# Two blocks of a network in one kernel: position tables stored with their keys backwards and read from a single DRAM copy

## The chip, the cores and the metric

The kernel runs on one core of a Trainium2 chip. The metric is the device time of one execution in microseconds. The core has five instruction streams: PE (matmuls; its weight loads are shown as PEld), DVE (elementwise work), ACT (activations, copies), POOL (small elementwise work; it also issues the DMAs of one queue) and SP (issues the DMAs of another). All DMAs share 16 DMA engines.

## The reference, cut to what matters

The program computes two blocks on 256 tokens of width 2048, in float32: a hybrid layer applied twice, then a second block with neighbourhood attention, four branches and a feed-forward part. The change touches only the attention biases, which depend on the distance between query and key.

In the first block, heads add a bias per distance to the scores and mask out later keys:

```python
dist = q_pos[:, None] - k_pos[None, :]
bias = bias_dist[jnp.clip(dist, 0, S - 1)]
s = s + jnp.transpose(bias, (2, 0, 1))[None, :, None]
s = jnp.where(dist >= 0, s, -jnp.inf)
```

So the bias of query q and key k is a function of q - k alone: the table of 128 queries by 256 keys holds one row of 384 values, shifted by one from each query to the next. There are 12 such rows (4 heads of one kind of attention, 8 of another). In the second block's neighbourhood attention, a head has a small table `rpb` by row and column distance; on a grid 64 columns wide its row of 127 values per row distance is shifted by one from each query column to the next in the same way.

## The kernel before, in words

Everything is arranged around a stream of weights. Each step of the program handles one piece of a weight matrix, 256 rows by 512 columns (512 KB). SP loads the piece into one of four `raw` buffers (line 335). ACT rounds it into `hi` (line 343), DVE takes `lo` = `raw` - `hi` (line 351), and PE multiplies with both halves: 12 matmuls of 128x512 a step, for two tiles of 128 tokens (lines 392 to 394). `hi` and `lo` are made up to four steps ahead of their use. A `raw` buffer is free for the next load when `lo` has been computed.

All else (attention heads, a depthwise convolution on DVE, norms, and a long matrix-vector product on DVE called `wmod`) is emitted as side tasks, a link per step, between the matmuls. The emission order is fixed when the program is built; each engine works through its own stream in order and waits on semaphores. A planner decides how much DVE work goes into a step: `Meter` (lines 55 to 76) adds up estimated times from the free sizes of the operands, and `room()` (line 177) says what is left in the step. The DMAs that POOL issues run as soon as POOL comes to them and their waits allow, which can be long before PE gets to that step.

The tables of the first block are made in `bias_tables`, a task that starts at step 20. A small matmul and an addition (line 548) give `r`, the 12 rows of 384 values. Line 551 writes them to DRAM 128 times over. Lines 553 to 556 read three tiles `T` of 4 heads each: partition p takes 256 values from copy p, starting one value earlier than partition p - 1. Such a DRAM row stands with key order ascending:

```python
scr = self.dp.tile([12, 128, 384], F32, name="scr")
nc.gpsimd.dma_start(scr, r.unsqueeze(1).broadcast_to([12, 128, 384]))
    nc.gpsimd.dma_start(t, bass.AP(scr.tensor, g * 4 * 128 * 384 + 127, [[383, 128], [128 * 384, 4], [1, 256]]))
```

The T loads wait for the landing of the write. `T` is used in `causal` (lines 841 and 843), where DVE adds it to the scores in PSUM and takes the minimum, twice per set of scores (256 and 128 columns).

For the second block, the function `tables` at step 220 (lines 1060 to 1064) copies the 56 rows of `rpb` 64 times over from DRAM to DRAM, and then loads a mask. In `na_head` each head has four small loads from that copy in two pairs (line 1261), and DVE subtracts the loaded values from the mask (line 1287).

Of the kernel before, what the change touches and what calls it, by code (L numbers as in the profile page):

```python
# [11 lines left out]
F32 = mybir.dt.float32  # L12
# [3 lines left out]
ALU = mybir.AluOpType  # L16
# [15 lines left out]
TAIL, END = 5, 3  # L32
# the order in which the normed (group, token tile) pieces are transposed, and how many a group's use waits for
TILES = [(0, 0), (1, 0), (0, 1), (1, 1), (2, 0), (2, 1), (3, 0), (3, 1)]
READY = [3, 4, 6, 8]
# the part of the program (in steps) over which each chunk of the modulation's product is spread
WMOD_STEPS = {0: (22, 146), 1: (160, 274), 3: (290, 380), 4: (380, 470), 2: (470, 552), 5: (552, 612)}
# [17 lines left out]
class Meter:  # L55
    """Passes calls on to an engine and adds up about how long they hold it, in us."""

# [29 lines left out]
class Task:  # L87
    """A generator that emits a side chain of the program, a link per step."""

# [23 lines left out]
class Block:  # L113
    """One block of output columns: all of its contraction, for its token tiles."""

# [13 lines left out]
class Kernel:  # L129
# [20 lines left out]

# [1 line left out]
    def s(self, shape, dt=F32, name="s"):  # L152
# [14 lines left out]

# [1 line left out]
    def add(self, gen, front=False, rows=2, banks=1):  # L169
# [7 lines left out]
    def room(self):  # L177
        """Time left on the vector engine until the tensor engine is through this step."""
        return self.t_pe + 2.6 - self.t_dve
# [4 lines left out]
    def need(self, t, items=1 << 30):  # L184
        """Emits what is left of a task (or its first items). A task between steps holds no more than
        its `rows` of the row buffers and its `banks` of the four, and what has begun stays within them."""
        if t.done or t.items >= items:
            return
        if t in self.tasks:
            self.tasks.remove(t)  # L190
        if t not in self.running:
            while self.held()[0] + t.rows > ROWS or self.held()[1] + t.banks > 4:
                self.need([r for r in self.running if not r.busy][0])
            self.running.append(t)
        was, t.forced = t.forced, True
        while not t.done and t.items < items:
            t.step()
        t.forced = was
        if t.done:
            self.running.remove(t)  # L200

    def wait(self, me, deps):
        """Lets steps pass until the tasks are done."""
        while not all(t.done for t in deps):
            if me().forced:
                for t in deps:
                    self.need(t)
                break
            yield
# [12 lines left out]

# [1 line left out]
    def rstd(self, var, n, scale, eps):  # L224
        """(var * scale + eps) ** -0.5 for [128, n]."""
        nc = self.nc
        r = self.m([128, 8], name="rstd", bufs=8)
        nc.gpsimd.tensor_scalar(r[:, 0:n], var, scale, eps, op0=ALU.mult, op1=ALU.add)
        nc.gpsimd.tensor_tensor(r[:, 0:n], r[:, 0:n], self.half[:, 0:n], op=ALU.pow)  # L229
        return r  # L230

    def split_t(self, items, ahead=0):
        """Transposes [128 tokens, 512] pieces and splits them. items: (src, hi, lo, scale, bias),
        src a function that gives the piece; scale and bias: [128, 4] columns or None."""
        nc = self.nc
        n = 0
# [64 lines left out]

# [1 line left out]
    def block(self, *args, **kw):  # L303
# [3 lines left out]
    def order(jobs):  # L307
        """Steps of four (job, half of its contraction, token tile) each, and the step after which each job's
        operands are free. At the tail of a block its first token tile goes ahead of the second."""
        units, i = [], 0  # L310
# [93 lines left out]

# [1 line left out]
    def wmod_init(self):  # L406
        """silu(c) @ w_mod + b_mod on the vector engine, 128 of its elements at a time."""
        self.wm_jobs = [(chunk, f, k) for chunk in (0, 1, 3, 4, 2, 5) for f in range(16) for k in range(2)]
# [95 lines left out]

# [1 line left out]
    def begin(self, load):  # L506
# [27 lines left out]
    def bias_tables(self):  # L534
# [9 lines left out]
        p = self.aux()  # L544
# [3 lines left out]
        nc.vector.tensor_tensor(r, p[0:12, 0:384], mk, op=ALU.add)  # L548
        # 128 copies of each row, read one short of their pitch: row p comes out shifted by p
        scr = self.dp.tile([12, 128, 384], F32, name="scr")  # L550
        nc.gpsimd.dma_start(scr, r.unsqueeze(1).broadcast_to([12, 128, 384]))
        self.T = []
        for g in (1, 2, 0):
            t = self.s([128, 4, 256], name="T")
            nc.gpsimd.dma_start(t, bass.AP(scr.tensor, g * 4 * 128 * 384 + 127, [[383, 128], [128 * 384, 4], [1, 256]]))
            self.T.append(t)
        self.T = [self.T[2], self.T[0], self.T[1]]

# [1 line left out]
    def layer(self, l):  # L560
# [217 lines left out]
    def rms_t(self, r, ss, sc, sh, dst=None, rs=None):  # L778
        """rms norm, scale and shift of token-major r (4 of [128, 2, 512]) into transposed halves."""
        nc = self.nc  # L780
# [37 lines left out]
    def qk_t(self, q, k, c, scale):  # L818
        """Transposed q (times scale) and k of one head: [128, 512], q then k."""
        nc = self.nc  # L820
# [13 lines left out]
    def causal(self, qk, rows, T, s, m, i):  # L834
        """Negated scores of both query tiles: [128, 384] (tile 1, then tile 0) and their minima."""
        nc = self.nc
# [3 lines left out]
        yield  # L840
        nc.vector.tensor_tensor_reduce(out=s[:, 0:256], in0=p[:, 0:256], in1=T, scale=1.0, scalar=3e38,
                                       op0=ALU.add, op1=ALU.min, accum_out=m[:, i:i + 1])
        nc.vector.tensor_tensor_reduce(out=s[:, 256:384], in0=p[:, 256:384], in1=T[:, 128:256], scale=1.0, scalar=3e38,
                                       op0=ALU.add, op1=ALU.min, accum_out=m[:, i + 1:i + 2])
# [9 lines left out]
    def pv(self, s, v, c):  # L854
        """Probabilities [128, 384] times v: PSUM [128, 256], tile 1 then tile 0."""
        nc = self.nc
# [130 lines left out]

# [1 line left out]
    def second(self):  # L989
# [70 lines left out]
        def tables():  # L1060
            self.rpb = self.dp.tile([56, 64, 127], F32, name="rpbs")
            nc.gpsimd.dma_start(self.rpb, a["rpb"].unsqueeze(1).broadcast_to([56, 64, 127]))
            self.mask = self.cp.tile([128, 64], F32, name="namask")
            nc.gpsimd.dma_start(self.mask, a["namask"])
# [168 lines left out]
    def context(self):  # L1233
        """Normed and modulated context, transposed and split."""
        nc, a = self.nc, self.a
# [13 lines left out]
    def na_head(self, j, hd, x, y, need, me):  # L1249
# [7 lines left out]
        def load(t):  # L1257
            raw = self.h([128, 256], name="rpb")
            for i in range(2):
                off = (hd * 7 + 3 - 2 * t - i) * 64 * 127 + 63  # L1260
                nc.gpsimd.dma_start(raw[i * 64:(i + 1) * 64, :].rearrange("p (a c) -> p a c", a=4),
                                    bass.AP(self.rpb.tensor, off, [[126, 64], [64 * 127, 4], [1, 64]]))
            return raw
# [15 lines left out]
        for t in range(2):  # L1279
# [8 lines left out]
                                    self.mask.unsqueeze(1).broadcast_to([128, 4, 64]),  # L1288
                                    raw.rearrange("p (a c) -> p a c", a=4), op=ALU.subtract)
            if t == 0:  # L1290
# [25 lines left out]
    def put_split(self, p, dst, c, scale=None):  # L1316
        """[128, 256] in PSUM into the halves of chunk c."""
        nc = self.nc
# [111 lines left out]

# [1 line left out]
def _bucket(d):  # L1432
# [6 lines left out]
def _constants():  # L1439
# [4 lines left out]
    oh[_bucket(np.maximum(d, 0)), j] = -1.0  # L1444
    c["onehot"] = oh
    mask = np.zeros((12, 384), np.float32)
    mask[:4] = np.where(d >= 0, 0.0, BIG)
    cnt = np.where(d >= 0, (d <= 128) + 1.0 * (d % 4 == 0) + 1.0 * (d % 16 == 0), 0.0)
    mask[4:] = np.where(cnt > 0, -np.log(np.maximum(cnt, 1.0)), BIG)
    c["dmask"] = mask  # L1450
    cc = np.arange(64)
# [20 lines left out]
def _layout(i):  # L1472
# [22 lines left out]
    def blocks(w):  # L1495
        """[.., K, N] as [.., N / 512, K / 256, 128, 1024]: what one transfer brings, in one piece."""
        k, m = w.shape[-2:]
# [8 lines left out]
        "dlam": n["diff_lambda"].reshape(DEPTH, 256), "gain": n["diff_head_gain"], "cols": cols,  # L1506
        "ln_g": n["ln_g"], "ln_b": n["ln_b"], "rel_bias": n["rel_bias"], "rpb": rpb.reshape(56, 127),
        "ctx": n["ctx_2"][0], "c": np.stack([n["c_2"][0], n["c_ctx_2"]]), "w_in2": blocks(n["w_in_2"][0]),
# [24 lines left out]
```

## Time and profile before

| | |
|---|---|
| device time, median of 3 runs | 2675.42 us (2675.05 to 2678.34) |
| profiled execution, first to last instruction (the span) | 2668.7 us; the page gives no other time for it |
| busy: PE, DVE, ACT, POOL | 2624.8, 1843.7, 1260.4, 126.1 us |
| `lo` (DVE, line 351), `hi` (ACT, line 343) | 1220 and 1059 ns each, 893 times |
| DMA moved | 616.79 MB, 231 GB/s over the span |
| DMA queue q0 (issued by POOL) | 11744 packets, 39.29 MB |
| time in DMA from issue to landing, a weight load | 4.4 us median |

Times in the rows below are microseconds from the start of the span unless marked ns. A matmul in the trace shows some 0.39 us because it overlaps with its neighbours; the distance from one start to the next is what it costs. The chain of work that ended last is followed back from the last instruction, at each step to what released it. Most of PE's matmuls have one line in the trace (line 75, the planner's wrapper), so they are told apart by tiles: `mm` is the weight stream, `aux` are the side tasks.

### The profile page before, as it was taken

What the parts mean: (1) busy time and instruction counts of PE and PEld (TensorE: products, weight loads), DVE (VectorE), ACT (ScalarE), POOL (GpSimd) and SP (SyncE); (2) the same over time, 40 slices, a digit from 0 to 9 for tenths busy, and PEclk for the clock granted to TensorE, in tenths of its full rate; (3) what the DMA queues carried; (4) which work ended last, traced back from release to release, by engine and by line L of the source; (5) the groups of instructions that cost most, each with busy time, mean ns of one, the idle gap of its engine ahead of it and who ended that gap; (6) DMA issues with size and microseconds to landing.
All of it is one profiled execution on the core that took longest, in us unless ns stands there. A gap on an engine that the chain in (4) does not pass through costs nothing.

```text
span 2668.7 us, 33167 instructions
## 1 busy us (share of the span) xinstructions
PE 2624.8 (98%) x11962; PEld 2164.3 (81%) x11962; DVE 1843.7 (69%) x3028; ACT 1260.4 (47%) x1609; POOL 126.1 (5%) x188
## 2 busy tenths in 40 slices
PE   9999999989999999999999999999999999999999
PEld 7788888768888888887888888888788888888887
DVE  5699787769988799664756686778554554555444
ACT  6354654435566556454454444444444434443442
POOL 0000010000000111020200000000100000000000
PEclk9999999999999999999999999999999999999999
DMA  8876667577765778785767787788655566556654
GB/s 304 213 231 219 212 225 251 194 221 233 233 227 195 280 268 286 255 256 184 230 224 237 255 283 260 262 289 305 222 181 190 190 237 205 189 190 240 225 194 154
DMA packets 171749, 616.79 MB, mean 231 GB/s; under 512 B 19994, under 2 KB 20788, under 8 KB 171584
## 3 DMA queue, kind: packets, MB, share of 16 engines
q1 hardware_dynamic: 158400, 572.59, 64.0%
q0 software_dynamic: 11744, 39.29, 5.3%
q10 hardware_dynamic: 1440, 2.79, 0.3%
q8 instruction: 94, 1.54, 0.2%
q14 instruction: 71, 0.58, 0.1%
HBM read 599.64 MB, written 16.76 MB: 231 GB/s over the span
## 4 chain that ended last, share of the span: by engine, by line
PE 87%; DVE 5%; DMA 4%; issue 2%; ACT 1%; POOL 0%; SPq 0%; ACTq 0%; DVEq 0%; POOLq 0%
PE mm L75 82%; PE aux L75 6%; DMA raw<-in_w_in 3%; DVE lo L351 2%; DVE f L75 1%; DVE wmjunk L75 1%; DVE cacc L75 1%; DMA raw<-in_w_out 1%; ACT hi L343 0%; DVE res L75 0%; DMA row<-in_ln_b 0%; DMA row<-in_ln_g 0%; DVE hcTl L75 0%; POOL rstd L229 0%; DVE bn L75 0%
## 5 line engine op out<-in xcount | busy, mean ns | idle before, releaser
L351 DVE TENSOR_TENSOR lo<-raw,hi 128x1024 fp32r<-128x1024 f32 (+1 forms) x893 | 1077.0, 1220 | 629.9 <-ACT hi L343 627.2
L343 ACT ACTIVATE hi<-raw 128x1024 fp32r<-128x1024 f32 (+1 forms) x893 | 937.5, 1059 | 1067.4 <-PE mm L75 777.7
L75 PE MATMUL mm<-hi,xTh 128*128 128x512 f32 x960 | 388.0, 404 | 18.3 <-ACT hi L343 18.3
L75 PE MATMUL mm<-lo,xTh 128*128 128x512 f32 x960 | 379.0, 395 | 3.5 <-DVE lo L351 3.5
L75 PE MATMUL mm<-hi,xTl 128*128 128x512 f32 x960 | 379.1, 395 | 0.6 <-DVE xTl L75 0.6
L75 DVE CUSTOM_DVE_ANT_0 wmjunk<-wm,c 128x512 bf16<-128x512 f32 x512 | 352.9, 689 | 13.1 <-DMA wm<-in_w_mod 1.9
L75 PE MATMUL mm<-hi,hTh 128*128 128x512 f32 x864 | 343.9, 398 | 0.0
L75 PE MATMUL mm<-hi,hTl 128*128 128x512 f32 x864 | 337.1, 390 | 0.0
L75 PE MATMUL mm<-lo,hTh 128*128 128x512 f32 x864 | 336.6, 390 | 0.0
L75 PE MATMUL mm<-hi,h2Th 128*128 128x512 f32 x704 | 275.9, 392 | 1.1 <-ACT h2Th L284 1.1
L75 PE MATMUL mm<-hi,h2Tl 128*128 128x512 f32 x704 | 274.4, 390 | 1.1 <-DVE h2Tl L75 1.1
L75 PE MATMUL mm<-lo,h2Th 128*128 128x512 f32 x704 | 274.2, 389 | 0.0
L75 PEld LDWEIGHTS mm<-hi,xTh 128*128 128x128 f32 x960 | 183.0, 191 | 57.9 <-ACT hi L343 20.0
L75 PEld LDWEIGHTS mm<-lo,xTh 128*128 128x128 f32 x960 | 183.2, 191 | 42.0 <-DVE lo L351 6.4
L75 PEld LDWEIGHTS mm<-hi,xTl 128*128 128x128 f32 x960 | 182.6, 190 | 40.5 <-DVE xTl L75 1.3
L75 PEld LDWEIGHTS mm<-hi,hTl 128*128 128x128 f32 x864 | 162.2, 188 | 34.5
L75 PEld LDWEIGHTS mm<-lo,hTh 128*128 128x128 f32 x864 | 162.5, 188 | 32.4 <-issue 0.2
L75 PEld LDWEIGHTS mm<-hi,hTh 128*128 128x128 f32 x864 | 162.4, 188 | 32.3 <-issue 0.2
L75 PEld LDWEIGHTS mm<-hi,h2Tl 128*128 128x128 f32 x704 | 132.2, 188 | 29.0 <-DVE h2Tl L75 1.5
L75 PEld LDWEIGHTS mm<-hi,h2Th 128*128 128x128 f32 x704 | 132.2, 188 | 28.3 <-ACT h2Th L284 1.6
L75 PEld LDWEIGHTS mm<-lo,h2Th 128*128 128x128 f32 x704 | 132.3, 188 | 26.9
L75 PE MATMUL mm<-hi,yTh 128*128 128x512 f32 x384 | 151.2, 394 | 0.0
(273 smaller groups left out, 3094.9 us busy)
## 6 DMA issues: line engine op xcount, KB each, us to landing
raw<-in_w_in SPq DMA_DIRECT2D x360, 512.0 KB, 4.4
wm<-in_w_mod SPq DMA_DIRECT2D x192, 512.0 KB, 4.7
raw<-in_w_gate SPq DMA_DIRECT2D x128, 512.0 KB, 4.5
raw<-in_w_fg SPq DMA_DIRECT2D x88, 512.0 KB, 4.3
raw<-in_w_fu SPq DMA_DIRECT2D x88, 512.0 KB, 3.9
raw<-in_w_fd SPq DMA_DIRECT2D x88, 512.0 KB, 4.2
raw<-in_w_out SPq DMA_DIRECT2D x64, 512.0 KB, 4.6
raw<-in_w_o SPq DMA_DIRECT2D x32, 512.0 KB, 5.1
```

The source lines that it names most:

```text
L75: return f(*args, **kw)
L343: nc.scalar.activation(hi[:, k], t[:, k], AF.Copy)
L351: nc.nc.vector.tensor_tensor(lo[:, k], t[:, k], hi[:, k], op=ALU.subtract)
```

## The change: what it does

The 12 rows and the `rpb` rows are stored with their keys backwards. Then the row of partition p starts one value *later* than that of partition p - 1, and 128 overlapping reads of one DRAM row, a step of one value apart, give the shifted table; a pitch of 383 over 128 copies is no longer needed. `scr` is 12 rows of 384 values (18 KB); the copy of `rpb` is dropped and the loads of `na_head` read the input itself. The tables in SBUF now hold their keys backwards, so DVE reads them with a step of -1 in three places. The constants (`onehot`, `dmask`) and `rpb` are reversed when the inputs are laid out. Comments are gone as well, which changes no instruction.

```diff
-        scr = self.dp.tile([12, 128, 384], F32, name="scr")
-        nc.gpsimd.dma_start(scr, r.unsqueeze(1).broadcast_to([12, 128, 384]))
+        scr = self.dp.tile([12, 384], F32, name="scr")
+        nc.gpsimd.dma_start(scr, r)
...
-            nc.gpsimd.dma_start(t, bass.AP(scr.tensor, g * 4 * 128 * 384 + 127, [[383, 128], [128 * 384, 4], [1, 256]]))
+            nc.gpsimd.dma_start(t, bass.AP(scr.tensor, g * 4 * 384 + 1, [[1, 128], [384, 4], [1, 256]]))
...
-        nc.vector.tensor_tensor_reduce(out=s[:, 0:256], in0=p[:, 0:256], in1=T, scale=1.0, scalar=3e38,
+        nc.vector.tensor_tensor_reduce(out=s[:, 0:256], in0=p[:, 0:256], in1=T[:, ::-1], scale=1.0, scalar=3e38,
...
-        nc.vector.tensor_tensor_reduce(out=s[:, 256:384], in0=p[:, 256:384], in1=T[:, 128:256], scale=1.0, scalar=3e38,
+        nc.vector.tensor_tensor_reduce(out=s[:, 256:384], in0=p[:, 256:384], in1=T[:, 0:128][:, ::-1], scale=1.0, scalar=3e38,
...
-            self.rpb = self.dp.tile([56, 64, 127], F32, name="rpbs")
-            nc.gpsimd.dma_start(self.rpb, a["rpb"].unsqueeze(1).broadcast_to([56, 64, 127]))
...
-                off = (hd * 7 + 3 - 2 * t - i) * 64 * 127 + 63
+                off = (hd * 7 + 3 - 2 * t - i) * 127
...
-                                    bass.AP(self.rpb.tensor, off, [[126, 64], [64 * 127, 4], [1, 64]]))
+                                    bass.AP(a["rpb"].tensor, off, [[1, 64], [127, 4], [1, 64]]))
...
-                                    raw.rearrange("p (a c) -> p a c", a=4), op=ALU.subtract)
+                                    raw.rearrange("p (a c) -> p a c", a=4)[:, :, ::-1], op=ALU.subtract)
...
-    c["onehot"] = oh
+    c["onehot"] = oh[:, ::-1]
...
-    c["dmask"] = mask
+    c["dmask"] = mask[:, ::-1]
```

## Rows read from the trace of the kernel before

**Rows 1.** The head of the page: span, then busy us of each engine.

```profile
span 2668.7 us, 33167 instructions
PE 2624.8 (98%) x11962; PEld 2164.3 (81%) x11962; DVE 1843.7 (69%) x3028; ACT 1260.4 (47%) x1609; POOL 126.1 (5%) x188
```

**Rows 2.** Timeline of PE, first stretch: start us, us, engine, line, operation, idle before.

```profile
75.74 0.39 PE L75 MATMUL mm<-lo,xTh 128*128 128x512 f32 x1
...
98.41 0.39 PE L75 MATMUL mm<-hi,xTl 128*128 128x512 f32 x1
99.89 0.50 PE L75 MATMUL mm<-hi,xTh 128*128 128x512 f32 x1 [1.10 <-ACT hi L343]
...
114.28 0.40 PE L75 MATMUL mm<-hi,xTl 128*128 128x512 f32 x1
```

**Rows 3.** The chain of work that ended last: start us, us, what.

```profile
84.80 26.66 DMA raw<-in_w_in
113.91 7.33 DMA raw<-in_w_in
565.53 25.66 DMA raw<-in_w_in
```

**Rows 4.** DMA issues: out<-in, queue, count, KB each, median us to landing.

```profile
c<-in_c ACTq DMA_DIRECT2D x4, 512.0 KB, 11.0
scr<-r POOLq DMA_DIRECT2D x1, 2304.0 KB, 36.4
rpb<-rpbs POOLq DMA_DIRECT2D x32, 64.0 KB, 5.7
rpbs<-in_rpb POOLq DMA_DIRECT2D x1, 1778.0 KB, 30.5
T<-scr POOLq DMA_DIRECT2D x3, 512.0 KB, 5.7
mk<-in_dmask POOLq DMA_DIRECT2D x1, 18.0 KB, 5.9
```

**Rows 5.** Instructions on `scr` and `rpbs`: duration ns min/median/max, first and last start.

```profile
L551 POOL DMA_DIRECT2D scr<-r x1: 1108/1108/1108, 75.3 to 75.3; - x1
...
L1062 POOL DMA_DIRECT2D rpbs<-in_rpb x1: 1718/1718/1718, 560.3 to 560.3; - x1
```

**Rows 6.** Busy us of PE, PEld, DVE, ACT, POOL; clock, DMA share, GB/s.

```profile
90.00:95.00 5.00, 5.00 (x23) 4.13 (x22) 2.02 (x3) 1.06 (x1) 0.00 (x0) 1.00 0.80 139
```

**Rows 7.** Timeline of PE, second stretch, columns as in rows 2.

```profile
578.93 0.39 PE L75 MATMUL mm<-hi,xTl 128*128 128x512 f32 x1
588.57 0.80 PE L75 MATMUL mm<-hi,xTh 128*128 128x512 f32 x1 [9.26 <-ACT hi L343]
...
593.73 0.40 PE L75 MATMUL mm<-hi,xTl 128*128 128x512 f32 x1
```

**Rows 8.** Timeline of PE, later places in the two layers, columns as in rows 2.

```profile
127.45 0.39 PE L75 MATMUL mm<-hi,xTh 128*128 128x512 f32 x1
128.46 0.50 PE L75 MATMUL mm<-lo,xTh 128*128 128x512 f32 x1 [0.62 <-DVE lo L351]
...
153.27 0.39 PE L75 MATMUL mm<-hi,xTl 128*128 128x512 f32 x1
...
156.33 0.48 PE L75 MATMUL mm<-hi,xTh 128*128 128x512 f32 x1
...
641.09 0.39 PE L75 MATMUL mm<-hi,xTl 128*128 128x512 f32 x1
...
642.59 0.48 PE L75 MATMUL mm<-hi,xTh 128*128 128x512 f32 x1
```

**Rows 9.** Instructions on tiles `sc`, `rpb`: ns min/median/max, first and last start, shapes.

```profile
L75 DVE CUSTOM_DVE_ANT_0 sc<-aux,T x64: 282/352/425, 153.0 to 849.0; 128x256 f32<-128x256 f32 x32, 128x128 f32<-128x128 f32 x32
L75 DVE TENSOR_SCALAR f<-aux,sc,sh x64: 389/397/408, 1014.1 to 1944.2; 128x128 f32<-128x128 f32 x64
...
L75 DVE TENSOR_TENSOR pad<-namask,rpb x16: 414/418/427, 1150.1 to 1410.5; 128x256 f32<-128x256 f32 x16
```

More of the change, by code (lines that the diff above doesn't have):

```diff
@@ L1506, in _layout @@
         "dlam": n["diff_lambda"].reshape(DEPTH, 256), "gain": n["diff_head_gain"], "cols": cols,
-        "ln_g": n["ln_g"], "ln_b": n["ln_b"], "rel_bias": n["rel_bias"], "rpb": rpb.reshape(56, 127),
+        "ln_g": n["ln_g"], "ln_b": n["ln_b"], "rel_bias": n["rel_bias"], "rpb": rpb[:, :, ::-1].reshape(56, 127),
         "ctx": n["ctx_2"][0], "c": np.stack([n["c_2"][0], n["c_ctx_2"]]), "w_in2": blocks(n["w_in_2"][0]),
```

## The prediction

> **What bounds the kernel now.** I read the head of the page first, then the chain that ended last, then the DMA issues, then the PE timeline around the places that stood out. PE is busy for 98% of the 2668.7 us span while DVE has 69% [rows 1], so a change off PE can only gain where PE is starved. Its steady rhythm is one 128x512 matmul every 0.2267 us: from the start at 75.74 to the one at 98.41 there are 100 intervals, 22.67 us [rows 2].
>
> The chain names two long links that are not PE: a weight load in flight for 26.66 us from 84.80, and another for 25.66 us from 565.53 [rows 3]. The DMA issues and their times say what else was in flight. The broadcast write `scr<-r` (2304 KB) goes out at 75.3 [rows 5] and takes 36.4 us, so to about 111.7; the weight load lands at 84.80 + 26.66 = 111.46. The broadcast write `rpbs<-in_rpb` (1778 KB) goes out at 560.3 [rows 5] and takes 30.5 us, to 590.8; the weight load lands at 591.19 [rows 3, 4]. Each pair agrees within half a microsecond; that is my evidence that these DRAM copies clog the engines that the weights share. While one is under way the DMA engines are 0.80 busy and move 139 GB/s in all, and DVE works 2.02 us of 5 [rows 6].
>
> What PE loses. First stretch: the last matmul on rhythm starts at 98.41, then 27 start late, the first at 99.89 and the last at 114.28; on rhythm the 27th would start at 98.41 + 27 x 0.2267 = 104.53, so 9.75 us are lost. Second stretch: 578.93 is on rhythm, 12 follow from 588.57 to 593.73, and on rhythm the 12th would start at 578.93 + 2.72 = 581.65: 12.08 us lost [rows 2, 7]. The lower clock during the restarts is inside both figures.
>
> **Part by part.**
>
> *The 128-fold copy goes.* `scr` becomes 18 KB. Its write costs about what the 18 KB load of the mask does, 5.9 us instead of 36.4 [rows 4], with twelve rows in place of 1536. The first clog vanishes, and with it 9.75 us. POOL's wait for the landing shrinks with it; nothing but the conv's later `rstd` is queued behind that wait on POOL, so it gives and costs nothing by itself.
>
> *The 64-fold copy goes.* One DMA of 1778 KB and the POOL slot that issues it go; the mask load behind it on the same queue lands sooner. The second clog vanishes: 12.08 us.
>
> *What follows the first clog.* After it DVE has lost its lead and PE pays twice more. A matmul at 128.46 follows one at 127.45, 0.78 over rhythm. Then nine transposes of the first heads' probabilities come late: from 153.27 to 156.33 is 3.06 us between the neighbouring matmuls, while the same nine in the second layer take 641.09 to 642.59, 1.50 us; 1.56 us over [rows 8]. Both are lateness of DVE, which stood idle more than half the time under the clog [rows 6]. Without the clog it keeps its lead, so I count both, 2.34 us; the other end is 0, if DVE would have been late anyway. The second layer's follow-up I put at 0, since that layer's transposes run undelayed already.
>
> *The three T loads move forward by about 30 us*, from the write's landing at 111.7 to about 75.3 + 1.1 + 5.9 = 82 [rows 4, 5]. Their sizes stay, 1 KB runs into 128 partitions, 1.5 MB together. What is new is that all of it is read from one region of 18 KB, and that it now falls beside weight loads that are in no distress yet. Their cost is not shown, so by bounds. Below: nothing, as the loads, where they stand now, land in 5.7 us and the weight load beside them in 7.33 us from 113.91 [rows 3, 4], and PE keeps its rhythm until 127.45. The cover is what the first clog shows: a weight load issued at 84.80 was not missed by PE before 98.64, 13.84 us later, less the two conversions. 7.33 us is well under it. Above: the slowest moving of such bulk on this queue, the `rpbs` write's 1778 KB in 30.5 us = 58 GB/s, which makes 1536 KB last 26.3 us. The row nearest in kind is `c<-in_c`: four loads of 512 KB, each reading one 4 KB row of DRAM for all 128 partitions, land in 11.0 us [rows 4], so a hot source as such does not choke the engines. I take 0. T is first used at 153.0 [rows 9], 60 us after it would land.
>
> *The 32 `rpb` loads* keep their size (64 KB, 256-byte runs, 5.7 us [rows 4]) and their place; they read 28 KB of DRAM in place of 1.8 MB. First use of the values is at 1150.1 [rows 9], behind PE work; 0 by the same argument.
>
> *The reversed operand.* 64 `sc` instructions (half of 256 columns, half of 128; median 0.352 us) and 16 `pad` instructions (256 columns, 0.418 us) now read one input backwards [rows 9]: 32 x 256 + 32 x 128 + 16 x 256 = 16384 columns, 64 x 0.352 + 16 x 0.418 = 29.2 us of DVE. No row has a negative step. Below: 0, the same words in the same number of columns; a gain I exclude, since nothing is read less. Above: the slowest float32 row per column, `f<-aux,sc,sh`, 128 columns in 0.397 us or 3.10 ns each [rows 9]; at that pace 16384 columns take 50.8 us, 21.6 more. I take 0, since the operands stay dense float32 of the same shapes. The program's own planner counts free sizes alone, so the order of instructions on each engine stays as it is.
>
> [...]
>
> **The sum.** 9.75 + 12.08 + 2.34 = 24.2 us, on the profiled execution's span: 2668.7 - 24.2 = 2644.5. That span lies 6.7 us under the 2675.42 us median of the runs shown (what is before the first and after the last instruction); I keep that as it is: 2651.2 us. What is late next is DVE: it is nearly full after each clog, but it no longer starts there with nothing in hand.
>
> **The rivals.**
>
> [...]
>
> *B. The T loads, read from one small region, clog in their turn.* From the two clogs: the losses plus the cover, 9.75 + 13.84 over 36.4 us and 12.08 + 13.6 over 30.5 us, are 0.65 and 0.84 us per us of clog; I take 0.75, so a clog of C us costs 0.75 C - 13.7. At the 58 GB/s pace C = 26.3 and 6.0 us come back: 2657.2. Against: the `c` loads.
>
> *C. Slower: the same place at the worst pace.* An `rpb` load moves 64 KB in 5.7 us, 11.2 KB per us. If reads of one DRAM spot go no faster however many are asked for, 1536 KB last 137 us: 0.75 x 137 - 13.7 = 89 us, 2740. It outweighs the gain as soon as C passes (24.2 + 13.7) / 0.75 = 51 us, that is under 30 KB per us for the T loads. The `c` loads, 2048 KB with a median landing of 11.0 us, speak strongly against it.
>
> *D. The change doesn't do what it says:* the weight loads are late for another reason (buffers freed late by DVE, whose work stands in the chain just ahead of both links), and the writes only happen to end together with them. Then 2675. Against: two landings that agree within half a microsecond, and 139 GB/s at 0.80 busy.
>
> **How the numbers follow.** Forecast as summed 0.68, with a range of its own of 2647 to 2655 (2.34 us less gained, and some 3 us either way for the estimate); A 0.13, B 0.10, C 0.04, D 0.05. The range 2646 to 2662 takes in the likeliest, B, and A up to half its upper end. About 0.2%, 5.4 us, is what a measurement of this kernel can tell from no change: faster by more holds in the forecast, A and B, 0.91; D is within, 0.05; C is slower, 0.04.
>
> **What would show it.** Right: no weight load of 20 us or more in the chain; `scr<-r` landing within about 6 us; no PE gap over 1 us between 85 and 160 or between 565 and 645; the nine transposes of the first layer within about 1.5 us; later events of the first layer about 12 us earlier, of the second about 24. [...] I am wrong if PE still stops for weights in those stretches, or if the gain at about 200 us is kept but lost again behind DVE by 900 us.

## The result, and the profile after

The changed kernel takes 2647.68 us (median; 2646.82 to 2648.27) against 2675.83 us (2675.05 to 2678.34) beside it: 28.15 us less, ratio 0.9897, 95% interval 0.9882 to 0.9911. The forecast was 2651.2 us, 24.2 us less. The profiled execution has a span of 2646.2 us and a time of 2647.96 us.

The head of the page, to be held against [rows 1]: PE's share of the span has gone from 98% to 99%.

```profile
span 2646.2 us, 33166 instructions
PE 2615.5 (99%) x11962; PEld 2161.0 (82%) x11962; DVE 1843.9 (70%) x3028; ACT 1260.5 (48%) x1609; POOL 125.1 (5%) x187
```

The chain that ended last, at the two places of [rows 3] (start us, us, what): where weight loads of 26 us stood, PE follows on PE.

```profile
71.22 49.21 PE mm L75 x216
...
537.37 57.15 PE mm L75 x252
```

The DMA issues that answer to [rows 4] (KB each, median us to landing). The two copies are gone, and the mask that was queued behind the second lands in 4.0 us. The T loads take 11.0 us instead of 5.7.

```profile
rpb<-in_rpb POOLq DMA_DIRECT2D x32, 64.0 KB, 5.7
T<-scr POOLq DMA_DIRECT2D x3, 512.0 KB, 11.0
namask<-in_namask POOLq DMA_DIRECT2D x1, 32.0 KB, 4.0
scr<-r POOLq DMA_DIRECT2D x1, 18.0 KB, 3.4
```

The mask's line before:

```profile
namask<-in_namask POOLq DMA_DIRECT2D x1, 32.0 KB, 29.3
```

Busy us of PE, PEld, DVE, ACT, POOL, then clock, DMA share and GB/s, in the stretches where the T loads now fall. In [rows 6] the DMA engines moved 139 GB/s at a share of 0.80; here they move 382 and 385 at 1.02 and 1.01, and PE is full.

```profile
85.00:90.00 5.00, 5.00 (x24) 4.14 (x23) 3.29 (x6) 1.97 (x2) 0.00 (x0) 1.00 1.02 382
90.00:95.00 5.00, 5.00 (x24) 4.14 (x23) 3.10 (x4) 1.21 (x2) 0.00 (x0) 1.00 1.01 385
```

The weight loads beside the T loads do take longer than their median of 4.4 us: the eight that are issued between 77 and 97 us land in 3.6 to 9.9 us, median 6.8.

PE at the nine transposes of [rows 8] (start us, us): from 142.42 to 143.55 is 1.13 us between the matmuls around them, where it was 3.06. DVE is ahead again: its first instruction on these scores starts at 135.4, 7.2 us before the transposes; before the change it started at 153.0 [rows 9], 1.1 us before the first of them.

```profile
142.42 0.40 PE L75 MATMUL mm<-hi,xTl 128*128 128x512 f32 x1
142.65 1.14 PE L75 MATMUL aux<-ident,sc 128*128 128x128 f32 x9
143.55 0.47 PE L75 MATMUL mm<-hi,xTh 128*128 128x512 f32 x1
```

The instructions that read backwards, to be held against [rows 9] (ns min/median/max): unchanged to within 2 ns in the median.

```profile
L75 DVE CUSTOM_DVE_ANT_0 sc<-aux,T x64: 282/352/426, 135.4 to 824.1; 128x256 f32<-128x256 f32 x32, 128x128 f32<-128x128 f32 x32
...
L75 DVE TENSOR_TENSOR pad<-namask,rpb x16: 415/420/426, 1128.9 to 1388.1; 128x256 f32<-128x256 f32 x16
```

Milestones show where the time came from. Three runs of matmuls stand in the chain of each kernel here: one of 60 in the attention of the first layer, its twin in the second layer, and one of 468 at the start of the second block. Before, and after:

```profile
362.96 13.65 PE mm L75 x60
849.22 13.65 PE mm L75 x60
1030.64 106.12 PE mm L75 x468
```

```profile
350.17 13.65 PE mm L75 x60
824.27 13.65 PE mm L75 x60
1008.17 106.12 PE mm L75 x468
```

The first comes 12.79 us earlier, the second 24.95, the third 22.47. Each clog gave 12 to 13 us; then this execution loses 2.48 us between the second layer and the second block, and keeps the rest to the end.

### The profile page after: what moved, and what is told of

The parts are those of the page before. It is cut to its first block, busy times and chain, and to the rows that moved or that the text cites. A ratio compares the mean times of both kernels' runs of the same rounds, so it can differ in the third digit from the quotient of the medians.

```text
span 2646.2 us, 33166 instructions
## 1 busy us (share of the span) xinstructions
PE 2615.5 (99%) x11962; PEld 2161.0 (82%) x11962; DVE 1843.9 (70%) x3028; ACT 1260.5 (48%) x1609; POOL 125.1 (5%) x187
## 4 chain that ended last, share of the span: by engine, by line
PE 92%; DVE 3%; DMA 2%; issue 1%; ACT 1%; POOL 0%; SPq 0%; ACTq 0%; DVEq 0%; POOLq 0%
PE mm L75 86%; PE aux L75 6%; DVE lo L351 1%; DMA raw<-in_w_out 1%; DMA raw<-in_w_in 1%; DVE f L75 1%; DMA row<-in_ln_b 1%; ACT hi L343 0%; DVE res L75 0%; DVE wmjunk L75 0%; POOL rstd L229 0%; DVE hcTl L75 0%; DVE bn L75 0%; POOL rstd L228 0%; DVE yTl L75 0%
## 5 line engine op out<-in xcount | busy, mean ns | idle before, releaser
L75 PE MATMUL mm<-hi,yTl 128*128 128x512 f32 x384 | 149.9, 390 | 1.6 <-DVE yTl L75 1.6
```

The costliest lines, as they stand in the source:

```text
L75: return f(*args, **kw)
```

## Experiments

Ratios are against the kernel before, run on the same chip.

**The kernel before again.** No edit.

> The kernel before, unchanged, to see where 4 of the measured 28 us sit that the sum (24.2 us) did not have: the change's own execution has only 1.8 us around its span, while 6.7 us lay between the span of the profile before and the median of its runs. Theory 1 (the clogs vary): the span of this execution is about 2673 to 2675 us, and PE loses some 28 us rather than 24 in the two stretches where the weight loads are late. Theory 2 (what lies around the span differs by the kernel): the span is again 2668 to 2669 us and the time 2675.

The profiled execution has a span of 2669.2 us and a time of 2670.92: theory 2 falls, 1.7 us lie around the span as in the changed kernel. But theory 1 isn't shown in this trace either. This execution is among the lowest of its ten (2670.59 to 2682.07, median 2674.17; the runs of the kernel before in the same session span 2669.62 to 2683.24), with the clogs at 36.2 and 31.2 us. So both profiles of this kernel show it some 3 to 5 us under its own median, and what an ordinary execution loses more isn't in them. The run with backwards copies, below, has a trace of an ordinary one.

**One table at a time.** The first kernel has the edits of `bias_tables` and `causal` alone, the second those of `tables` and `na_head` alone.

> Only the first block's table is changed (12 rows once in DRAM, read backwards); the 64-fold copy of rpb stays. The clog theory expects half the gain: some 12 to 14 us under the kernel before (ratio 0.995), no PE gap between 85 and 160 us, and the gap of about 12 us near 570 us unchanged. If buffers freed late by DVE were the cause, the time stays within 3 us of the kernel before.

> Only the second block's table is changed (rpb read from the input, backwards); the 128-fold copy stays. The clog theory expects 12 to 15 us under the kernel before (ratio 0.995), the gap after 98 us as before and none near 580 us; with the run that has the other half the gains should add up to that of the whole change within 3 us. The rival of late buffers expects no change of over 3 us.

The first: 2662.18 us (2657.80 to 2665.61), ratio 0.9950 (0.9935 to 0.9965). The second: 2661.16 us (2659.46 to 2665.19), ratio 0.9950 (0.9935 to 0.9964). Against 2674.79 beside them that is 12.6 and 13.6 us less, 26.2 together; the whole change gave 28.15 in its own session and 26.2 in a later one. The chain of each keeps the one long weight load whose copy it keeps (first table only, then second only):

```profile
549.30 23.56 DMA raw<-in_w_in
```

```profile
85.13 27.61 DMA raw<-in_w_in
```

PE doesn't wait at all between 60 and 165 us in the first, and waits 0.6 us in all between 540 and 650 in the second. The two parts are independent and add up within the 3 us that were expected.

**Copies that nobody reads.** The changed kernel and

```diff
+        junk = self.dp.tile([12, 128, 384], F32, name="junk")
+        nc.gpsimd.dma_start(junk, r.unsqueeze(1).broadcast_to([12, 128, 384]))
...
+            self.rpb = self.dp.tile([56, 64, 127], F32, name="rpbs")
+            nc.gpsimd.dma_start(self.rpb, a["rpb"].unsqueeze(1).broadcast_to([56, 64, 127]))
```

> The changed kernel with both broadcast writes put back into DRAM tiles that nothing reads (2304 KB and 1778 KB); the tables are still read from the single copies. The clog theory expects nearly all of the gain to go: within 5 us of the kernel before. If the gain came from what the loads wait for or read (T earlier, reads from a small region), it expects to stay within 3 us of the changed kernel, 28 us faster.

2675.62 us (2670.78 to 2680.06), ratio 1.0003 (0.9993 to 1.0012): all of the gain goes, with nothing that depends on the copies. The copies alone are the cost. The first stretch costs somewhat more than before (the first milestone stands at 365.84, where the kernel before has 362.96); the T loads now queue behind the copy and land in 36.4 us, which is the likely reason. In its windows PE starves as before:

```profile
95.00:100.00 5.00, 4.39 (x20) 3.30 (x18) 0.00 (x0) 0.00 (x0) 0.00 (x0) 1.00 0.80 152
100.00:105.00 5.00, 0.64 (x1) 0.29 (x1) 0.67 (x1) 1.06 (x1) 0.00 (x0) 0.77 0.78 126
```

**Backwards, with the copies.** The changed kernel with both folds kept, and the pitch one longer instead of one shorter. Cut to the read of the first table; the `rpb` loads are changed in the same way:

```diff
...
-            nc.gpsimd.dma_start(t, bass.AP(scr.tensor, g * 4 * 384 + 1, [[1, 128], [384, 4], [1, 256]]))
+            nc.gpsimd.dma_start(t, bass.AP(scr.tensor, g * 4 * 128 * 384 + 1, [[385, 128], [128 * 384, 4], [1, 256]]))
...
```

> Keys backwards and the three reversed reads on DVE as in the change, but both folds of copies kept in DRAM (read with a pitch one longer instead of one shorter). If the whole gain is the copies, the time is that of the kernel before, within 4 us, and the DVE instructions on T and on the rpb values keep 0.35 and 0.42 us. [...]

2674.65 us (2670.88 to 2677.65), ratio 1.0002 (0.9992 to 1.0012). The reversed instructions have medians of 350 and 419 ns, where [rows 9] has 352 and 418 for forward reads. Rival A, that DVE reads backwards more slowly, is out: reading backwards is free here.

```profile
L75 DVE CUSTOM_DVE_ANT_0 sc<-aux,T x64: 280/350/425, 152.4 to 847.5; 128x256 f32<-128x256 f32 x32, 128x128 f32<-128x128 f32 x32
...
L75 DVE TENSOR_TENSOR pad<-namask,rpb x16: 414/419/428, 1154.5 to 1414.0; 128x256 f32<-128x256 f32 x16
```

The profiled execution took 2673.93 us, 0.7 under the median of its runs, so it is an ordinary one, with both copies. Its three milestones:

```profile
362.41 13.65 PE mm L75 x60
847.74 13.65 PE mm L75 x60
1034.09 106.12 PE mm L75 x468
```

Held against the profile after, the two clogs cost 12.24 and 11.23 us here, no more than in the profile before (12.79 and 12.16). What makes this execution longer lies between the last two milestones: 186.35 us, where the profile before has 181.42.

**The same bytes in long rows.** The kernel before with

```diff
+        one = self.dp.tile([12, 384], F32, name="one")
+        nc.gpsimd.dma_start(one, r)
-        scr = self.dp.tile([12, 128, 384], F32, name="scr")
-        nc.gpsimd.dma_start(scr, r.unsqueeze(1).broadcast_to([12, 128, 384]))
+        scr = self.dp.tile([128, 12 * 384], F32, name="scr")
+        nc.gpsimd.dma_start(scr, bass.AP(one.tensor, 0, [[0, 128], [1, 12 * 384]]))
...
+            self.rpb = self.dp.tile([64, 56 * 127], F32, name="rpbs")
+            nc.gpsimd.dma_start(self.rpb, bass.AP(a["rpb"].tensor, 0, [[0, 64], [1, 56 * 127]]))
...
```

> The kernel before with the same bytes copied, but in long rows: scr as 128 copies of all 12 rows one after the other (18 KB runs, DRAM to DRAM from one small write), rpb as 64 copies of the whole 28 KB table. If the bytes are what clogs, 2.3 and 1.8 MB still take over 25 us each and the time stays within 6 us of the kernel before. If the short rows (1536 and 508 bytes) are, the copies land in under 15 us, PE does not stop, and the time is within 5 us of the changed kernel.

2646.56 us (2644.64 to 2649.80), ratio 0.9892 (0.9873 to 0.9910): as fast as the changed kernel, with every copied byte still there and T read forwards. The copies land in 12.9 and 10.8 us:

```profile
scr<-one POOLq DMA_DIRECT2D x1, 2304.0 KB, 12.9
...
rpbs<-in_rpb POOLq DMA_DIRECT2D x1, 1778.0 KB, 10.8
```

So the bytes don't clog; the way they were copied did. Two runs look for what in it.

**Short rows again, in two ways.** First with the copies outermost, as above, but gaps between the rows; then in the order of the kernel before, with `scr` copied from DRAM and the `rpb` rows padded to 128 values, in the input as well as in the copy. Both are cut to the copies; the reads of T and of the `rpb` values follow the layout.

```diff
...
+        scr = self.dp.tile([128, 12, 400], F32, name="scr")
+        nc.gpsimd.dma_start(scr[:, :, 0:384], bass.AP(one.tensor, 0, [[0, 128], [384, 12], [1, 384]]))
...
+            self.rpb = self.dp.tile([64, 56, 128], F32, name="rpbs")
+            nc.gpsimd.dma_start(self.rpb[:, :, 0:127], bass.AP(a["rpb"].tensor, 0, [[0, 64], [127, 56], [1, 127]]))
...
```

```diff
...
+        scr = self.dp.tile([12, 128, 384], F32, name="scr")
+        nc.gpsimd.dma_start(scr, bass.AP(one.tensor, 0, [[384, 12], [0, 128], [1, 384]]))
...
+            self.rpb = self.dp.tile([56, 64, 128], F32, name="rpbs")
+            nc.gpsimd.dma_start(self.rpb, a["rpb"].unsqueeze(1).broadcast_to([56, 64, 128]))
...
```

> As the run with long rows (scr from one small DRAM copy; copies outermost in DRAM), but with gaps between the rows, so that each run is again 1536 bytes (scr) and 508 bytes (rpb). If the length of the runs is what makes the copies slow, scr takes over 25 us and rpbs over 20 us to land, PE stops in both stretches, and the time is within 8 us of the kernel before. If it is the order (copy outermost in place of row outermost) or DRAM as the source, both land in under 15 us and the time is that of the run with long rows, 2647 us.

> The order of the kernel before (row outermost), with scr copied from one small DRAM copy instead of from SBUF (runs of 1536 bytes as before), and rpb rows padded to 128 values, so runs of 512 bytes instead of 508. If the SBUF source was what slowed scr, it lands in under 20 us now; if not, in 30 us or more. If the 508 bytes were what slowed rpbs, it lands in under 20 us now; if not, in 25 us or more. Where both stay slow, the time is that of the kernel before within 4 us.

2647.30 us (ratio 0.9893, 0.9874 to 0.9913) and 2648.28 us (0.9896, 0.9882 to 0.9911). Both keep PE fed in the two stretches, but for one wait of 0.8 us in the second. With the copies outermost both landed a little later than the 15 us that were expected, and far under the 25 and 20 us of the other theory. Copies outermost, then rows of 512 bytes:

```profile
scr<-one POOLq DMA_DIRECT2D x1, 2304.0 KB, 16.8
...
rpbs<-in_rpb POOLq DMA_DIRECT2D x1, 1778.0 KB, 16.9
```

```profile
scr<-one POOLq DMA_DIRECT2D x1, 2304.0 KB, 16.8
...
rpbs<-in_rpb POOLq DMA_DIRECT2D x1, 1792.0 KB, 19.4
```

For `scr` the cause is shown to be the source: the same DRAM layout in the same order of the same 1536-byte rows takes 16.8 us from DRAM and 36.4 from SBUF [rows 4], where it lies in 12 partitions. The DMA queues say what that does to the weights (packets, MB, share of the time of the 16 engines; q0 carries the copy and T loads, q1 the weights). Before, from 75.3 to 112 us, then with `scr` copied from DRAM, from 75 to 112 us:

```profile
q0 software_dynamic: 704, 2.36, 57.4%
q1 hardware_dynamic: 925, 3.38, 24.6%
```

```profile
q1 hardware_dynamic: 1876, 6.83, 52.4%
q0 software_dynamic: 1168, 3.95, 29.8%
```

Out of SBUF, q0 held more than half of the engines' time for 2.36 MB; from DRAM it moved more in half of that time, and the weights got twice as much through. The short rows go with the 4 us between 12.9 and 16.8, which both layouts of 1536-byte rows took. For `rpbs`, a run of 508 bytes as such isn't slow either (16.9 us); slow are 508-byte rows laid end to end in the old order, and making them 512 bytes long, and so 512 apart, brings 30.5 down to 19.4. Whether alignment or length does that is not separated: the padded run changes both, and in the input that is read as well as in the copy.

**One spot or spread.** The changed kernel; before the last T load, the same tile is loaded alternately from 2 MB of a weight matrix and from T's own 6 KB of DRAM (four rows of 383 values; the 4.6 KB in the expectation below are too few), each load after the one before has landed.

```diff
+            for i in range(4 if g == 0 else 0):
+                nc.gpsimd.dma_start(t, bass.AP(a["w_fd"].tensor, 1 + i * 1048576, [[4097, 128], [1024, 4], [1, 256]]))
+                if i < 3:
+                    nc.gpsimd.dma_start(t, bass.AP(scr.tensor, g * 4 * 384 + 1, [[1, 128], [384, 4], [1, 256]]))
```

> The changed kernel; before the last T load the same tile is loaded seven times more, one load after the other, alternately from a stretch of 2 MB of a weight matrix (rows 16 KB apart) and from the 4.6 KB of DRAM that T comes from; the same shape, 1 KB runs. In the changed kernel T loads land in 11.0 us (median) against 5.7 before. If reading one spot is slow, the loads from it land in 10 us or more and the spread ones in 5 to 7. If the company of the weight loads and of each other was the cause, both kinds land alike, in 4 to 8 us, and differ by under 1.5 us in the median.

2646.11 us, one run. The timeline of POOL, where each issue waits for the landing before it:

```profile
92.42 0.75 POOL L559 DMA_DIRECT2D T<-scr  x1 [10.77 <-DMA T<-in_w_fd]
99.84 0.75 POOL L557 DMA_DIRECT2D T<-in_w_fd  x1 [6.68 <-DMA T<-scr]
104.35 0.75 POOL L559 DMA_DIRECT2D T<-scr  x1 [3.76 <-DMA T<-in_w_fd]
111.13 0.75 POOL L557 DMA_DIRECT2D T<-in_w_fd  x1 [6.02 <-DMA T<-scr]
118.89 0.75 POOL L559 DMA_DIRECT2D T<-scr  x1 [7.01 <-DMA T<-in_w_fd]
126.03 0.75 POOL L557 DMA_DIRECT2D T<-in_w_fd  x1 [6.39 <-DMA T<-scr]
134.64 0.75 POOL L560 DMA_DIRECT2D T<-scr  x1 [7.86 <-DMA T<-in_w_fd]
```

From issue to issue, loads from one spot took 7.4, 6.8 and 7.1 us, spread ones 4.5, 7.8 and 8.6 (medians over all six and all four: 7.1 and 7.9). One spot isn't slower. The spread load that is not listed above went out at 80.9, right behind two other T loads, and took 11.2 us, so the 11.0 us go with three loads at once beside weights. Rivals B and C are out: in the profile after, PE doesn't wait at all between 60 and 165 us.

**Half a copy.** The changed kernel with an unread 64-fold copy in place of 128.

> The changed kernel with a 64-fold copy of the 12 rows written as well and read by nobody (1152 KB, half of the first clog). The prediction's model, in which PE has 13.7 us of cover and then loses 0.75 us per us, expects 18 us in flight and no loss: within 2 us of the changed kernel, 2647 to 2650 us. A loss in proportion to the copy expects half of the 13 us that the second-table-only run lost against the changed kernel: about 2654 us.

2651.93 us (2649.90 to 2653.00): 4.2 us over the changed kernel in its first session and 5.5 over it in a later one, between the two expectations, so neither holds as put. In the trace 4.77 us are lost by the first milestone (354.94, where the profile after has 350.17). The copy is issued at 77.5 and lands in 19.2 us, at 96.7. A weight load stays in flight for much longer (start us, us):

```profile
85.65 19.88 DMA raw<-in_w_in
```

It lands at 105.53, 6.0 us over the cover of 13.84. The model of rival B, 0.75 C - 13.7 with the copy's own 19.2 us as C, gives 0.7 us where 4.2 to 4.8 were lost, so it fails as it stands. The likely reason is that it counts the copy alone: the T loads queue behind the copy and land in 21.4 us, so the clog lasted longer. No run has the half copy without them.

**The changed kernel again, and a norm moved.** The second kernel is

```diff
                 def gen():
-                    yield
+                    for _ in range(2 if key == "kc0" else 1):
+                        yield
                     ss = self.m([128, 8], name="qss")
```

> The changed kernel, unchanged, for the spread of its executions and for the stretch between the two blocks (from the last head of the second layer to the long run of matmuls that follows), which took 181.2 to 186.4 us in the profiles so far, with and without the copies. If only the clogs made the kernel before vary by 13 us, these executions stay within 3 us of each other. If that stretch varies by itself, they spread over 5 us.

> The changed kernel; the first key norm of the context is emitted one step later, so that on POOL its two operations come behind the two that the second block's input waits for. In profiles with the long stretch, PE waits 2.7 to 3.4 us there for a scaling that waits for POOL. If that wait is what varies, the time is 1 to 4 us under the changed kernel (ratio 0.999 against it), PE's wait at that place is under 1 us, and the stretch takes 181 us or less. If it is not, the times are alike.

The changed kernel: 2646.40 us (2644.07 to 2648.67; 2672.61 beside it, ratio 0.9905, 0.9885 to 0.9925). The spread is 4.6 us over four executions, between the two expectations; the kernel before has 9.2 over the seven beside it, and 13.6 over nineteen in an earlier session. That the spread went with the copies is likely, but so few executions don't show how much of it did. Its stretch between the second and third milestone took 181.61 us, against 183.90 in the first profile of the same kernel. POOL there, first in the profile after, then in this one:

```profile
978.87 2.66 POOL L229 TENSOR_TENSOR rstd<-rstd,half 128x8 f32<-128x8 f32 x1
981.62 1.22 POOL L228 TENSOR_SCALAR rstd<-tot 128x1 f32<-128x1 f32 x1
982.93 1.41 POOL L229 TENSOR_TENSOR rstd<-rstd,half 128x1 f32<-128x1 f32 x1
```

```profile
977.11 1.68 POOL L229 TENSOR_TENSOR rstd<-rstd,half 128x8 f32<-128x8 f32 x1
978.88 0.25 POOL L228 TENSOR_SCALAR rstd<-tot 128x1 f32<-128x1 f32 x1
979.21 1.01 POOL L229 TENSOR_TENSOR rstd<-rstd,half 128x1 f32<-128x1 f32 x1
```

The same three instructions take 5.3 or 2.9 us of POOL, and PE waits 2.7 or 0.5 us on the scaling behind them. The long form also stands in the run with backwards copies, where the stretch took 186.35 us, and in the half copy, so it isn't the change that brings it. What makes POOL slower in some executions is open. With the norm moved: 2644.96 us (2643.23 to 2647.64; ratio 0.9899, 0.9883 to 0.9916), no wait of PE at that place and a stretch of 181.45 us, where 181 or less were expected. It is 1.4 us under its neighbour, but the ranges overlap and its own spread is 4.4 us: no version is shown to beat the changed kernel.

## Why the prediction was right, point by point

- **The clogs.** Right, in cause and size. The first stretch gave 12.79 us where 9.75 + 2.34 = 12.09 were forecast, the second 12.16 where 12.08 were. That the second came within 0.1 us is luck: the same stretch took 471.3 to 475.0 us in the profiles without the second clog. Rival D is out by the unread copies.
- **What follows the first clog.** Right: PE doesn't wait between 60 and 165 us, and the nine transposes take 1.13 us, 1.93 less than before where 1.56 were counted.
- **The T loads.** Right at nothing for PE. The argument leant on a weight load of 7.33 us beside them; the longest took 9.9, still within the cover of 13.84. The T loads themselves land in 11.0 us, not 5.7, and the small write in 3.4, not 5.9.
- **The reversed operand.** Right at nothing: the `sc` instructions took 352 ns forwards and backwards, the `pad` instructions 418 and 420. The chance of 0.13 for rival A and the end of the range at 2662 us stand on a slower backwards read, which no run shows.
- **From span to median.** This is the step that failed in size: "That span lies 6.7 us under the 2675.42 us median [...]; I keep that as it is". Only 1.7 us lie around a span; the other 5 were a profiled execution that ran faster inside than its median. The forecast of the span, 2644.5 us, was good: the two profiles of the changed kernel have 2646.2 and 2643.7, the first with 2.48 us more between the blocks than the profile before, which nothing in the change caused. So the forecast of the time came out 3.5 us too high: 5.2 us too much around the span, 1.7 us too little in it. Between profiles the gain was 22.5 us, between medians 28.15, and 26.2 in the later session. The few us by which the medians gain more than the traced clogs (23.5 to 25 us) are not shown to come from the change. The run with backwards copies, which has the trace of an ordinary execution, has clogs of the usual size and a longer stretch between the blocks, and such a stretch stands in profiles of the changed kernel too. Why the medians still differ by more stays open.
- **The reason why the copies cost.** The prediction blamed traffic of DRAM copies as such, and took 139 GB/s at 0.80 busy as a mark of clogging. It was one: the engines were held by a slow transfer, 57.4% of their time for 2.36 MB. But copies as large, laid out in another way or read from DRAM, cost nothing that shows in the times (2646.56 to 2648.28 us). The forecast was right without knowing that.

## What to carry to other kernels

A bulk copy beside a tight weight stream is to be judged by its rate, not its bytes: 2.3 MB at 65 GB/s starved PE, the same 2.3 MB in 12.9 us did not. Read share and GB/s of the DMA engines together; a high share with low GB/s (here 0.80 with 139, where the changed kernel has 1.02 with 382) marks the transfer to reshape, and where it can't go, reading it from DRAM or in longer rows (here 16.8 and 12.9 us in place of 36.4) may do as much as removing it. Before a gain of 1% is added up from one profile, set that execution's own time against the median of its kernel.

## What the runs showed of the hardware that was not expected

- A DMA out of 12 SBUF partitions moved 2304 KB at 65 GB/s (36.4 us) and 1152 KB at 61 GB/s (19.2 us); from DRAM, into the same layout, the 2304 KB took 16.8 us. Whether the number of partitions sets the 65 GB/s is not shown; no run here varies it.
- 508-byte rows laid end to end: 30.5 us for 1778 KB; 508-byte runs 512 bytes apart, copies outermost: 16.9 us; 512-byte rows end to end, in the order of the first: 19.4 us for 1792 KB.
- Many partitions reading one spot of DRAM (6 KB): 7.1 us for 512 KB, against 7.9 us spread over 2 MB.
- DVE reading float32 with a step of -1, from SBUF beside a PSUM or an SBUF operand: no change (352 and 418 to 420 ns).
